# Queries and keys of a two-layer decoder computed with the tokens stationary, rotated as [tokens, columns] and turned through memory; other PSUM banks for the feed-forward

## The chip, the cores and the metric

The kernel runs on one core of one Trainium2 chip. The metric is the device time of one execution in microseconds (us), the median of several executions. A core has TensorE (PE, with a row of its own, PEld, for the loading of the stationary operand), VectorE (DVE), ScalarE (ACT), GpSimd (POOL) and SyncE (SP, which here does nothing but issue transfers).

## The reference, cut to what matters

Two layers over 256 tokens of width 2048, all float32. Each layer projects the normalised input to the q, k and v of four groups of 4 heads x 128, runs four kinds of causal attention on them, projects the result out and applies a SwiGLU feed-forward of width 5632.

```
for l in range(2):
    h = rmsnorm(x, attn_norm[l])
    z = h @ w_in[l]                      # q, k, v of fox, moba, diff, sb: 12 pieces of 512 columns, and 4 gate columns
    fox  = softmax(q k^T / sqrt(128) + gates, causal) v
    moba = softmax(rope(q) rope(k)^T / sqrt(128), causal) v
    diff = rmsnorm((softmax(rope(q1) rope(k1)^T / 8) - lam softmax(rope(q2) rope(k2)^T / 8)) v)
    sb   = stick_breaking(q, k) v
    x = x + concat(fox, moba, diff, sb) @ w_out[l]
    h = rmsnorm(x, ffn_norm[l])
    x = x + (silu(h @ w_gate[l]) * (h @ w_up[l])) @ w_down[l]
return rmsnorm(x, final_norm)
```

rope turns the two halves of a head (of half a head in diff) against each other: x1 cos - x2 sin and x2 cos + x1 sin.

## The kernel before

**Blocks.** All weights lie in memory as blocks of 128 x 1024 float32 (512 KB), in the order in which they are used. SP loads each into `raw` (L193, 4 buffers). ACT rounds it to `hi` (L202) and DVE forms the rest `lo = raw - hi` (L203), 3 buffers each; `run_ahead` does this for the two blocks after the current one. Activations have the same two halves (`xh`). Each product is three matmuls, hi by lo, lo by hi and hi by hi, in float32r.

**Products.** Three forms stand in the kernel. `rows_block` (L388, matmuls L399 to L401) holds 128 tokens stationary and streams 512 weight columns; it makes v, the output projection and most of the down projection, 12 matmuls of 512 columns to a block. `gate_up_product` (L405, matmuls at L417) does the same for gate and up. `pair_product` (L357, L369 to L371) makes q and k the other way round: 128 weight columns are stationary and the 256 tokens stream, 24 matmuls of 256 columns to a block, so that q and k come out as [columns, tokens], as the scores want them. There are 8 blocks to each of q, k and v of a group, so 16 q and k products in the two layers.

**Order.** A layer does v, q, k of diff, then q, k, v of moba, fox and sb, then the output projection, 11 chunks of gate and up, and the down projection. After each block `tick()` takes one step of three queues of side work, each written as a generator that yields between its steps: `evacs` (what empties PSUM), `background` (the attention of the groups, one group after the other) and `spare` (the forget gate). All engines work through their instructions in the order in which this program issues them. `OUT_ORDER` takes two blocks of the second output chunk ahead of the blocks that need the sb heads; if these aren't there, `source` finishes `background` on the spot.

**Emptying q and k.** `rope_pair` (L477) multiplies a pair of heads in PSUM by tables that already hold cos and sin times the norm's factor (`rope`, L351, made from a product with a diagonal, L327), and then combines the pieces in 8 (diff) or 4 (moba) small operations (L491, L492). `plain_pair` (L494) is one multiplication for fox and sb.

**Turning through memory.** `turn_steps` (L422) turns a [tokens, columns] result to [columns, tokens]: DVE transposes 32 x 32 pieces (L427), one step later SP writes 512 KB to memory (L430), two steps later SP reads it back in four transfers (L435), and two steps later it is used. Before the change this is done for the 22 chunks of act and the 14 of the output and down projections.

**PSUM.** Eight banks, four under the tag `mm` and four under `at`. The products take `mm`, the attention `at`. Gate and up alternate, chunk 0 in `mm` (L986: `("mm", "at")[c % 2]`); the norm's small sums are in `at`. So chunk 0 follows the last output product in `mm`, and the first down product follows chunk 10 in `mm`.

Of the kernel before, what the change touches and what calls it, by code (L numbers as in the profile page):

```python
# [19 lines left out]
P = 128  # L20
# [19 lines left out]
FG0 = 3 * GW  # L40
HEAD0 = {"fox": 0, "moba": 4, "diff": 8, "sb": 12}
# [7 lines left out]
def pair_columns(name, which, hp):  # L49

    c0 = COL0[name] + (0 if which == "q" else GW) + hp * 2 * HD
    base = c0 + np.arange(2 * HD).reshape(2, HD)
    if name == "moba":
        h = base.reshape(2, 2, 64)
        return h.transpose(1, 0, 2).reshape(-1)
    if name == "diff":
        h = base.reshape(2, 2, 2, 32)
        return h.transpose(2, 0, 1, 3).reshape(-1)
    return base.reshape(-1)
# [3 lines left out]
C_COS = {"moba": 0, "diff": 512}  # L63
C_ID = 1024
# [12 lines left out]
def constants():  # L77
    c = np.zeros((P, C_ALL), np.float32)
    pos = np.arange(S, dtype=np.float32)
    for name, dim in (("moba", HD), ("diff", HD // 2)):  # L80
        inv = (1.0 / (np.float32(10000.0) ** (np.arange(0, dim, 2, dtype=np.float32) / np.float32(dim)))).astype(np.float32)
        ang = (pos[:, None] * inv[None, :]).astype(np.float32)
        r = P // (dim // 2)
        c[:, C_COS[name]:C_COS[name] + S] = np.tile(np.cos(ang).T, (r, 1))
        c[:, C_COS[name] + S:C_COS[name] + 2 * S] = np.tile(np.sin(ang).T, (r, 1))
# [18 lines left out]
def lay_out(inp):  # L104
# [15 lines left out]
    for l in range(DEPTH):  # L120
# [9 lines left out]
        for kind, what, nb in plan():  # L130
            if what[0] != l:
                continue
            if kind == "pair":
                put(w_in, every, pair_columns(*what[1:]), 256)
            elif kind == "v":
                c0 = COL0[what[1]] + 2 * GW
                put(w_in, every, slice(c0, c0 + GW), 512)
# [21 lines left out]
def plan():  # L159

    out = []
    for l in range(DEPTH):
        for g in ORDER:
            pairs = [("pair", (l, g, which, hp), 4) for which in ("q", "k") for hp in range(2)]
            v = [("v", (l, g), 8)]
            out += v + pairs if g == ORDER[0] else pairs + v
# [8 lines left out]
def trunk(ctx: ExitStack, tc: tile.TileContext, x_t, vec, w, consts, y_t):  # L175
# [43 lines left out]
    for b, (to, of, c0, c1) in enumerate([(con, consts, C_ID, C_KEEP), (con, consts, 512, C_ID), (con, consts, 0, 512),  # L219
                                          (vecs, vec, V_GF, V_ALL)]):  # L220
        beside[NJ // 2 + b] = [(to[:, c0:c1], of[:, c0:c1])]
# [97 lines left out]
    def diag_product(cols):  # L319

        diag = tp.tile([P, 2, P], F32, name="diag", tag="diag", bufs=1)
# [8 lines left out]
    def norm_steps():  # L330
        acc = state["acc"]
        yield
        pst = ps.tile([P, 512], F32, name="pss", tag="at")
# [9 lines left out]
    def attn_norm_steps(l):  # L343
        yield from norm_steps()
        pbc = yield from diag_product(state["rcol"])
        rbc = tp.tile([P, S], F32, name="rbc", tag="rbc", bufs=1)
        A.activation(rbc, pbc[:, :S], AF.Copy)
        state["rbc"] = rbc
        rope = tp.tile([P, 4, S], F32, name="rope", tag="back", bufs=1)
        for n in range(4):  # L350
            V.tensor_tensor(rope[:, n], con[:, n * S:(n + 1) * S], rbc, op=ALU.mult)  # L351
        state["rope"] = {"moba": (rope[:, 0], rope[:, 1]), "diff": (rope[:, 2], rope[:, 3])}
# [4 lines left out]
    def pair_product(src):  # L357

        nonlocal block
        out = ps.tile([P, 2, S], F32, name="pp", tag="mm")  # L360
        for kb in range(4):
            run_ahead(block)
            hi, lo = halves.pop(block)
            for kk in range(4):
                k = kb * 4 + kk
                xk = src[k]
                for c in range(2):
                    at = kk * 256 + c * P
                    T.matmul(out[:, c], hi[:, at:at + P], xk[:, S:], start=k == 0 and c == 0, stop=False)  # L369
                    T.matmul(out[:, c], lo[:, at:at + P], xk[:, :S], start=False, stop=False)  # L370
                    T.matmul(out[:, c], hi[:, at:at + P], xk[:, :S], start=False, stop=k == NJ - 1 and c == 1)  # L371
            block += 1
            tick()
        return out

    def v_product():
        nonlocal block
        outs = [ps.tile([P, GW], F32, name=f"pv{t}", tag="mm") for t in range(2)]
# [43 lines left out]
    def turn_steps(get):  # L422
# [10 lines left out]
        back = tp.tile([P, 8, 4, 32], F32, name="back", tag="back", bufs=1)  # L433
# [43 lines left out]
    def rope_pair(name, out, hp, pp):  # L477
        cos, sin = state["rope"][name]
        both = tp.tile([P, 2, 2, S], F32, name="mcs", tag="tr", bufs=1)
        mc, ms = both[:, 0], both[:, 1]  # L480
        V.tensor_tensor(mc, pp, cos[:, None, :].to_broadcast([P, 2, S]), op=ALU.mult)
        V.tensor_tensor(ms, pp, sin[:, None, :].to_broadcast([P, 2, S]), op=ALU.mult)
        n = 64 if name == "moba" else 32
        yield
        for i in range(P // n):
            if i * n == 64:
                yield
            r = slice(i * n, (i + 1) * n)
            h = 2 * hp + i * n // 64
            to = 0 if name == "moba" else 64 * (i % 2)  # L490
            V.tensor_tensor(out[to:to + n, h], mc[r, 0], ms[r, 1], op=ALU.subtract)  # L491
# [583 lines left out]
```

## Time and profile before

| | before |
|---|---|
| median of 3 runs | 2290.41 us (2288.62 to 2291.55) |
| the profiled execution's own time | 2288.27 us |
| its span | 2286.5 us |
| granted TensorE clock, mean | 0.994 |
| PE busy | 2253.4 us (99%) |
| DVE busy | 1329.5 us (58%) |
| ACT busy | 1040.0 us (45%) |
| POOL busy | 224.3 us (10%) |
| moved by DMA | 456.47 MB, 200 GB/s |

The span is what the profiler saw of the program; 1.8 us of the execution's own time lie around it. Matmuls overlap each other, and their ends are modelled, so the time that one takes is read from the distance between the starts of two that follow each other, not from its own duration. Busy shares are means over the whole span; the attention, the output projection and the feed-forward have different limits.

### The profile page before, as it was taken

How to read it: one execution, taken by the hardware profiler on the slowest of the kernel's cores; microseconds unless marked ns; L12 is line 12 of the kernel's file. 1: busy time of each engine (PE TensorE's matmuls, PEld its weight loads, DVE VectorE, ACT ScalarE, POOL GpSimd, SP SyncE). 2: the span in 40 equal slices, each digit the busy share in tenths (PEclk: the TensorE clock that was granted, in tenths of full speed). 3: DMA queues.
4: the chain of work that ended last, by engine and by line, in shares of the span. 5: the costliest groups of instructions: out<-in, count | busy, mean ns of one | idle time of the engine just before them, and what ended most of it. 6: DMA issues, size and time to landing. Idle time of an engine off the chain costs nothing.

```text
span 2286.5 us, 30240 instructions
## 1 busy us (share of the span) xinstructions
PE 2253.4 (99%) x11801; PEld 1932.1 (85%) x11801; DVE 1329.5 (58%) x1524; ACT 1040.0 (45%) x1284; POOL 224.3 (10%) x206
## 2 busy tenths in 40 slices
PE   9999999999999999999999999999999999999997
PEld 7989988788888887888899899887888888878887
DVE  7995546555555555455569855565555555554444
ACT  6444454444444444444443444554444444444443
POOL 3570001100000000000007500010000000000001
PEclk9999999999999999999999999999999999999999
DMA  7554457667667666666654444576766766766673
GB/s 251 168 165 154 157 165 228 204 214 228 212 212 230 211 212 218 211 209 210 200 181 162 160 156 163 167 230 198 233 212 211 226 216 212 224 209 203 212 219 130
DMA packets 165744, 456.47 MB, mean 200 GB/s; under 512 B 15968, under 2 KB 53600, under 8 KB 165600
## 3 DMA queue, kind: packets, MB, share of 16 engines
q1 hardware_dynamic: 165168, 454.01, 62.5%
q8 instruction: 92, 1.51, 0.3%
q10 hardware_dynamic: 432, 0.53, 0.1%
q14 instruction: 52, 0.43, 0.1%
HBM read 433.50 MB, written 20.97 MB: 199 GB/s over the span
## 4 chain that ended last, share of the span: by engine, by line
PE 88%; DVE 7%; DMA 2%; issue 1%; ACT 1%; SPq 0%; DVEq 0%
PE gate L417 21%; PE up L417 21%; PE po L399 6%; PE po L400 6%; PE po L401 6%; PE pp L369 4%; PE pp L370 4%; PE pp L371 4%; PE po L458 3%; DVE lo L203 2%; PE pv L400 2%; PE pv L401 2%; PE pv L399 2%; PE po L459 1%; DMA back<-mem 1%
## 5 line engine op out<-in xcount | busy, mean ns | idle before, releaser
L203 DVE TENSOR_TENSOR lo<-raw,hi 128x1024 fp32r<-128x1024 f32 (+1 forms) x785 | 963.4, 1229 | 896.6 <-ACT hi L202 888.2
L202 ACT ACTIVATE hi<-raw 128x1024 fp32r<-128x1024 f32 (+1 forms) x785 | 829.6, 1059 | 1130.7 <-PE up L417 513.2
L417 PE MATMUL gate<-hi,xh 128*128 128x512 f32 x1408 | 550.5, 391 | 7.2 <-DVE tr L427 6.9
L417 PE MATMUL up<-hi,xh 128*128 128x512 f32 x1408 | 549.9, 391 | 0.0
L417 PEld LDWEIGHTS gate<-hi,xh 128*128 128x128 f32 x1408 | 265.6, 189 | 63.7 <-DVE tr L427 7.8
L417 PEld LDWEIGHTS up<-hi,xh 128*128 128x128 f32 x1408 | 265.5, 189 | 55.6 <-DVE tr L427 0.6
L369 PE MATMUL pp<-xh,hi 128*128 128x256 f32 x1024 | 292.4, 286 | 0.0
L370 PE MATMUL pp<-xh,lo 128*128 128x256 f32 x1024 | 289.9, 283 | 1.0 <-DVE lo L203 1.0
L371 PE MATMUL pp<-xh,hi 128*128 128x256 f32 x1024 | 289.7, 283 | 0.0
L417 PE MATMUL gate<-lo,xh 128*128 128x512 f32 x704 | 275.1, 391 | 1.1 <-DVE lo L203 1.1
L417 PE MATMUL up<-lo,xh 128*128 128x512 f32 x704 | 274.8, 390 | 0.0
L302 POOL TENSOR_TENSOR acc<-acc,sq 128x256 f32<-128x256 f32 x73 | 68.5, 938 | 1913.0 <-ACT sq L301 1910.3
L399 PE MATMUL po<-hi,act 128*128 128x512 f32 x528 | 205.6, 389 | 3.4 <-ACT g L964 3.4
L400 PE MATMUL po<-lo,act 128*128 128x512 f32 x528 | 205.4, 389 | 0.0
L401 PE MATMUL po<-hi,act 128*128 128x512 f32 x528 | 205.4, 389 | 0.0
L370 PEld LDWEIGHTS pp<-xh,lo 128*128 128x128 f32 x1024 | 196.4, 192 | 1.6 <-DVE lo L203 1.4
L369 PEld LDWEIGHTS pp<-xh,hi 128*128 128x128 f32 x1024 | 196.4, 192 | 0.2
L371 PEld LDWEIGHTS pp<-xh,hi 128*128 128x128 f32 x1024 | 196.3, 192 | 0.0
L417 PEld LDWEIGHTS gate<-lo,xh 128*128 128x128 f32 x704 | 132.8, 189 | 29.5 <-DVE lo L203 1.9
L417 PEld LDWEIGHTS up<-lo,xh 128*128 128x128 f32 x704 | 132.7, 189 | 27.5
L399 PEld LDWEIGHTS po<-hi,act 128*128 128x128 f32 x528 | 99.1, 188 | 24.8 <-ACT g L964 4.3
L401 PEld LDWEIGHTS po<-hi,act 128*128 128x128 f32 x528 | 99.1, 188 | 20.6
(225 smaller groups left out, 2391.8 us busy)
## 6 DMA issues: line engine op xcount, KB each, us to landing
raw<-w SPq DMA_DIRECT2D x783, 512.0 KB, 4.2
mem<-tr SPq DMA_DIRECT2D x36, 512.0 KB, 4.9
back<-mem SPq DMA_DIRECT2D x144, 128.0 KB, 4.7
x_all<-x_t SPq DMA_DIRECT2D x7, 256.0 KB, 6.9
y_t<-x_all SPq DMA_DIRECT2D x4, 256.0 KB, 3.0
con<-consts SPq DMA_DIRECT2D x3, 256.0 KB, 4.6
raw<-w SPq DMA_DIRECT2D x2, 256.0 KB, 3.5
y_t<-x_all SPq DMA_DIRECT2D x4, 128.0 KB, 2.3
```

Source lines behind the costliest of these rows:

```text
L202: A.activation(hi[:, c], raw[:, c], AF.Copy)
L203: V.tensor_tensor(lo[:, c], raw[:, c], hi[:, c].bitcast(F32), op=ALU.subtract)
L302: G.tensor_tensor(state["acc"], state["acc"], sq, op=ALU.add)
L369: T.matmul(out[:, c], hi[:, at:at + P], xk[:, S:], start=k == 0 and c == 0, stop=False)
L370: T.matmul(out[:, c], lo[:, at:at + P], xk[:, :S], start=False, stop=False)
L371: T.matmul(out[:, c], hi[:, at:at + P], xk[:, :S], start=False, stop=k == NJ - 1 and c == 1)
L399: T.matmul(outs[t], xlo, wh, start=first, stop=False)
L400: T.matmul(outs[t], xhi, wl, start=False, stop=False)
L401: T.matmul(outs[t], xhi, wh, start=False, stop=last)
L417: T.matmul(outs[n][t], st, wt[:, n * GC:(n + 1) * GC], start=first, stop=last)
L458: T.matmul(outs[n][c], hi[:, at:at + P], xk, start=k == 0, stop=False)
L459: T.matmul(outs[n][c][:, S:], lo[:, at:at + P], xk[:, :S], start=False, stop=end)
```

## The change

The 16 q and k products use `rows_block`, as v did, so they come out as [tokens, columns] in two PSUM banks, and `pair_product` is gone. `q_or_k_steps` empties them: for moba and diff four multiplications by the norm's factor and a table of cos or sin, and two operations that combine the halves; for fox and sb two ACT copies with the factor as scale. The result is turned by `turn_steps`. The operand that the scores hold stationary (q for fox, moba and diff, k for sb) is read back to `back` and copied by ACT to [head, token] order. The other is read back straight into its tile and streamed by the score matmuls through a pattern (`by_heads`) whose runs are 32 elements long, 128 elements apart. The product with a diagonal and the scaled tables are no longer made for the attention. The unscaled tables are larger: their three loads have 256, 256 and 512 KB in place of 256 KB each. In the feed-forward chunk 0 of gate and up, and so chunk 10 too, takes `at`, and the norm's sums take `mm`.

```diff
-    def pair_product(src):
...
-    def v_product():
-        nonlocal block
-        outs = [ps.tile([P, GW], F32, name=f"pv{t}", tag="mm") for t in range(2)]
+    def in_product():
+        outs = [ps.tile([P, GC], F32, name=f"in{t}", tag="mm") for t in range(2)]
         for kb in range(8):
             rows_block(x_source, outs, kb, 8)
         return outs
...
-    def rope_pair(name, out, hp, pp):
...
+    def q_or_k_steps(name, which, outs, to, ready):
+
+        z = tp.tile([P, 2, GC], F32, name="z", tag="g", bufs=1)
+        if name in TABLES:
+            at, n = TABLES[name]
+            halves_of = lambda a: a.rearrange("p (s h n) -> p s h n", h=2, n=n)
+            ms = tp.tile([P, 2, GC], F32, name="ms", tag="tr", bufs=1)
+            for m, out in enumerate((z, ms)):
+                for t in range(2):
+                    tab = con[:, at + (2 * m + t) * n:at + (2 * m + t) * n + n]
+                    V.scalar_tensor_tensor(out[:, t].rearrange("p (s n) -> p s n", n=n),
+                                           outs[t].rearrange("p (s n) -> p s n", n=n), state["rcol"][:, t:t + 1],
+                                           tab[:, None, :].to_broadcast([P, GC // n, n]), op0=ALU.mult, op1=ALU.mult)
+            yield
+            zh, mh = (a.rearrange("p t (s h n) -> p (t s) h n", h=2, n=n) for a in (z, ms))
+            V.tensor_tensor(zh[:, :, 0], zh[:, :, 0], mh[:, :, 1], op=ALU.subtract)
+            V.tensor_tensor(zh[:, :, 1], zh[:, :, 1], mh[:, :, 0], op=ALU.add)
         else:
-            V.scalar_tensor_tensor(out[:, 2 * hp:2 * hp + 2], pp, scale, rbc, op0=ALU.mult, op1=ALU.mult)
-        yield
+            r = state["rq" if which == "q" else "rcol"]
+            for t in range(2):
+                A.activation(z[:, t], outs[t], AF.Copy, scale=r[:, t:t + 1])
+        yield
+        if which == STATIONARY[name]:
+            new = yield from turn_steps(lambda t: z[:, t])
+            A.activation(to.rearrange("p h (a n) -> p h a n", n=32), new, AF.Copy)
+            yield
+        else:
+            yield from turn_steps(lambda t: z[:, t], to.rearrange("p h s -> p (h s)").rearrange("p (a h n) -> p a h n", h=NH, n=32))
+        ready[which] = True
...
-            T.matmul(s0[:, h], q[:, h, :P], k[:, h, :P], start=h == 0, stop=False)
+            T.matmul(s0[:, h], q[:, h, :P], k[:, h, :4], start=h == 0, stop=False)
...
             def pairs():
-                for which in ("q", "k"):
-                    for hp in range(2):
-                        pp = pair_product(xh)
-                        if name in ("moba", "diff"):
-                            evacs.append(rope_pair(name, qk[which], hp, pp))
-                        else:
-                            evacs.append(plain_pair(qk[which], hp, pp, HD ** -0.5 if which == "q" else None))
-                evacs.append(mark(ready))
+                for which in "qk":
+                    evacs.append(q_or_k_steps(name, which, in_product(), qk[which], ready))
...
-        evacs.append(norm_steps())
+        evacs.append(norm_steps("mm"))
         for c in range(NFC):
-            evacs.append(act_steps(c, *gate_up_product(("mm", "at")[c % 2])))
+            evacs.append(act_steps(c, *gate_up_product(("at", "mm")[c % 2])))
```

PE, early in the first q product of layer 0; `pp` and `in` are the product's PSUM tiles, `xh` the tokens, `hi` and `lo` the weights. Before:

```order
L369 MATMUL pp<-xh_118,hi_330 128x256
L370 MATMUL pp<-xh_118,lo_331 128x256
L371 MATMUL pp<-xh_118,hi_330 128x256
L369 MATMUL pp<-xh_125,hi_330 128x256
L370 MATMUL pp<-xh_125,lo_331 128x256
L371 MATMUL pp<-xh_125,hi_330 128x256
```

After:

```order
L371 MATMUL in_377<-hi_330,xh_118 128x512
L372 MATMUL in_377<-lo_331,xh_118 128x512
L373 MATMUL in_377<-hi_330,xh_118 128x512
L371 MATMUL in_378<-hi_330,xh_118 128x512
L372 MATMUL in_378<-lo_331,xh_118 128x512
L373 MATMUL in_378<-hi_330,xh_118 128x512
```

Before, the 256 tokens of a tile `xh` stream past 128 weight columns and then past the next 128 (the first three rows are the second half of `xh_118`); after, 128 tokens of it are held while all 512 weight columns stream, and then the other 128.

PE, output projection of layer 0, from the last products of the sb attention (`po<-t,v`) to the next weight block; `mix0` to `mix7` are the mixed heads, `mix6` and `mix7` those of sb. Before:

```order
L558 MATMUL po_3525<-t0_3299,v_2709 128x256
L559 MATMUL po_3525<-t1_3300,v_2709 128x128
L399 MATMUL po0_3443<-hi99_3483,mix3_2482 128x512
L400 MATMUL po0_3443<-lo99_3484,mix3_2482 128x512
L401 MATMUL po0_3443<-hi99_3483,mix3_2482 128x512
L399 MATMUL po1_3444<-hi99_3483,mix3_2482 128x512
```

After:

```order
L536 MATMUL po_2888<-t0_2672,v_2087 128x256
L537 MATMUL po_2888<-t1_2673,v_2087 128x128
L371 MATMUL po0_2688<-hi104_2822,mix6_2893 128x512
L372 MATMUL po0_2688<-lo104_2823,mix6_2893 128x512
L373 MATMUL po0_2688<-hi104_2822,mix6_2893 128x512
L371 MATMUL po1_2689<-hi104_2822,mix6_2893 128x512
```

Before, a block that reads the heads of another group (`mix3`) follows the sb products, and `mix6` is first read after several more; after, the block that follows reads `mix6`, which ACT and DVE make from those very products. Between the matmuls that finish the sb scores, which three Exp operations of ACT then read, and these products stand two weight blocks before the change and one after it.

SP, in the q and k products of layer 0: weight loads alone before,

```order
L193 DMA raw_1168<-w 128x1024
L193 DMA raw_1209<-w 128x1024
L193 DMA raw_1249<-w 128x1024
L193 DMA raw_1294<-w 128x1024
L193 DMA raw_1331<-w 128x1024
```

and after, with the k of diff being turned:

```order
L190 DMA raw_813<-w 128x1024
L402 DMA mem<-tr 128x2x512
L190 DMA raw_837<-w 128x1024
L190 DMA raw_859<-w 128x1024
L408 DMA k<-mem 32x8x128 x4
L190 DMA raw_885<-w 128x1024
```

The write `mem<-tr` and the four reads `k<-mem` now stand in the queue of the weight loads, two loads apart.

## Rows read from the trace of the kernel before

**Rows 1.** The page, part 1: busy time, share of the span, instructions.
```profile
PE 2253.4 (99%) x11801; PEld 1932.1 (85%) x11801; DVE 1329.5 (58%) x1524; ACT 1040.0 (45%) x1284; POOL 224.3 (10%) x206
```

**Rows 2.** Waits of PE: who waited for whom, total us, times, longest us.
```profile
PE gate L417 <- DVE tr L427: 6.9, 2, 3.5
PE pv L400 <- DVE lo L203: 3.8, 4, 1.4
PE po L399 <- ACT g L964: 3.4, 2, 1.7
```

**Rows 3.** Timeline, PE, 20 to 39 us: start, us, what was run.
```profile
20.25 0.39 PE L401 MATMUL pv<-hi,xh 128*128 128x512 f32 x1
...
31.13 0.39 PE L401 MATMUL pv<-hi,xh 128*128 128x512 f32 x1
...
33.07 0.28 PE L369 MATMUL pp<-xh,hi 128*128 128x256 f32 x1
...
38.35 0.28 PE L371 MATMUL pp<-xh,hi 128*128 128x256 f32 x1
```

**Rows 4.** Timeline, PE, start of the feed-forward of layer 0.
```profile
412.84 0.40 PE L417 MATMUL up<-hi,xh 128*128 128x512 f32 x1
416.70 0.80 PE L417 MATMUL gate<-hi,xh 128*128 128x512 f32 x1 [3.46 <-DVE tr L427]
...
422.57 0.40 PE L417 MATMUL up<-hi,xh 128*128 128x512 f32 x1
```

**Rows 5.** Windows: stretch, PE, PEld, DVE, ACT, POOL busy, granted clock, DMA.
```profile
416.70:422.20 5.50, 5.50 (x13) 4.17 (x14) 1.76 (x2) 1.06 (x1) 0.00 (x0) 0.50 0.75 255
```

**Rows 6.** Timeline, DVE, the same place as rows 4.
```profile
413.67 2.35 DVE L203 TENSOR_TENSOR lo<-raw,hi 128x1024 fp32r<-128x1024 f32 x2
415.94 1.30 DVE L427 STREAM_TRANSPOSE tr<-po 128x512 f32<-128x512 f32 x2
```

**Rows 7.** Timeline, PE, end of gate and up of layer 0.
```profile
897.24 0.39 PE L417 MATMUL up<-hi,xh 128*128 128x512 f32 x1
899.35 0.50 PE L399 MATMUL po<-hi,act 128*128 128x512 f32 x1 [1.72 <-ACT g L964]
```

**Rows 8.** Groups by form, DVE: busy us, mean ns, idle before.
```profile
L481 DVE TENSOR_TENSOR mcs<-pp,rope 128x512 f32<-128x512 f32 x16 | 10.9, 681 | 0.0
L491 DVE TENSOR_TENSOR q<-mcs 64x256 f32<-64x256 f32 x8 | 5.3, 663 | 0.1
L965 DVE SCALAR_TENSOR_TENSOR g<-up,rcol,g 128x512 f32<-128x512 f32 x44 | 30.9, 744 | 1.6 <-ACT g L964 1.6
L427 DVE STREAM_TRANSPOSE tr<-g 128x512 f32<-128x512 f32 x44 | 28.5, 687 | 0.0
```

**Rows 9.** Windows: a stretch of the attention of layer 0.
```profile
100.00:145.00 45.00, 42.26 (x314) 38.69 (x313) 44.24 (x71) 21.05 (x44) 41.91 (x35) 1.00 0.43 141
```

**Rows 10.** Timeline, stick-breaking group of layer 0, its last steps.
```profile
324.31 0.60 ACT L806 ACTIVATE t<-z 128x512 f32<-128x512 f32 x1
...
330.10 0.60 PE L558 MATMUL po<-t,v 128*128 128x256 f32 x2
...
331.19 0.38 PE L559 MATMUL po<-t,v 128*128 128x128 f32 x2
331.22 0.68 DVE L565 TENSOR_TENSOR mix<-po,mix 128x512 fp32r<-128x512 f32 x1
```

**Rows 11.** Waits (ACT and SP), then the DMA issues of the page.
```profile
ACT act L973 <- DMA back<-mem: 15.6, 14, 2.6
...
SPq L435 <- DMA mem<-tr: 19.8, 24, 2.6
...
back<-mem SPq DMA_DIRECT2D x144, 128.0 KB, 4.7
```

**Rows 12.** Groups by form, ACT.
```profile
L973 ACT ACTIVATE act<-back 128x512 fp32r<-128x512 f32 x44 | 27.3, 621 | 15.8 <-DMA back<-mem 15.6
...
L788 ACT ACTIVATE h<-n 128x512 fp32r<-128x512 f32 x2 | 1.2, 614 | 0.0
```

More of the change, by code (lines that the diff above doesn't have):

```diff
@@ L40 @@
 FG0 = 3 * GW
+STATIONARY = {"fox": "q", "moba": "q", "diff": "q", "sb": "k"}
 HEAD0 = {"fox": 0, "moba": 4, "diff": 8, "sb": 12}
@@ L46, in turned, with columns @@
     return np.arange(n).reshape(n // GC, 4, 4, 32).transpose(0, 2, 1, 3).reshape(-1)
[L49 to L64, printed above, removed]
+def columns(name, which):
+    c0 = COL0[name] + "qkv".index(which) * GW
+    order = np.arange(GW)
+    if which != "v":
+        order = order.reshape(NH, 4, 32).transpose(1, 0, 2).reshape(-1)
+    return c0 + order
+TABLES = {"moba": (0, 256), "diff": (1024, 128)}
+C_ID = 1536
 C_ONE = C_ID + P
@@ L132, in lay_out @@
                 continue
[L133 to L137, printed above, removed]
+            if kind == "in":
+                put(w_in, every, columns(*what[1:]), GC)
             elif kind == "out":
@@ L163, in plan @@
         for g in ORDER:
-            pairs = [("pair", (l, g, which, hp), 4) for which in ("q", "k") for hp in range(2)]
-            v = [("v", (l, g), 8)]
-            out += v + pairs if g == ORDER[0] else pairs + v
+            out += [("in", (l, g, which), 8) for which in ("vqk" if g == ORDER[0] else "qkv")]
         out += [("out", (l, c, kb), 1) for c, kb in OUT_ORDER]
@@ L344, in attn_norm_steps @@
         yield from norm_steps()
[L345 to L352, printed above, removed]
-    block = 0
-    def pair_product(src):
-        nonlocal block
[L360 to L374, printed above, removed]
-    def v_product():
-        nonlocal block
-        outs = [ps.tile([P, GW], F32, name=f"pv{t}", tag="mm") for t in range(2)]
+        rq = tp.tile([P, 2], F32, name="rq", tag="rq")
+        V.tensor_scalar(rq, state["rcol"], HD ** -0.5, None, op0=ALU.mult)
+        state["rq"] = rq
+    block = 0
+    def in_product():
+        outs = [ps.tile([P, GC], F32, name=f"in{t}", tag="mm") for t in range(2)]
         for kb in range(8):
@@ L420, in gate_up_product, with turn_steps @@
         return outs
-    def turn_steps(get):
+    def turn_steps(get, back=None):
         tr = tp.tile([P, 2, GC], F32, name="tr", tag="tr", bufs=1)
@@ L432, in turn_steps @@
         yield
-        back = tp.tile([P, 8, 4, 32], F32, name="back", tag="back", bufs=1)
+        if back is None:
+            back = tp.tile([P, 8, 4, 32], F32, name="back", tag="back", bufs=1)
         for g in range(4):
@@ L475, in tmp @@
         return big.tile(shape, dtype, name=name, tag=f"t{n}")
-    def rope_pair(name, out, hp, pp):
[L478 to L483, printed above, removed]
-        yield
-        for i in range(P // n):
-            if i * n == 64:
-                yield
[L488 to L491, printed above, removed]
-            V.tensor_tensor(out[to + n:to + 2 * n, h], mc[r, 1], ms[r, 0], op=ALU.add)
@@ L679, in score_steps @@
                 qu, ku = units[n * i + c]
-                T.matmul(s0[i][:, c], qu[:, :P], ku[:, :P], start=c == 0, stop=False)
+                T.matmul(s0[i][:, c], qu[:, :P], ku[:, :4], start=c == 0, stop=False)
         for c in range(n):
@@ L765, in sb_steps @@
         for h in range(NH):
-            T.matmul(z1[:, h], k[:, h, P:], q[:, h, P:], start=h == 0, stop=h == NH - 1)
+            T.matmul(z1[:, h], k[:, h, P:], q[:, h, 4:], start=h == 0, stop=h == NH - 1)
         yield
@@ L852, in attention @@
             at = 3 * (n % 2)
-            qk = {"q": tmp(at, [P, NH, S], "q"), "k": tmp(at + 1, [P, NH, S], "k")}
+            qk = {which: tmp(at + i, [P, NH, S], which) for i, which in enumerate("qk")}
             vt = tmp(at + 2, [P, 2, GW], "v")
@@ L857, in v_part @@
             def v_part():
-                outs = v_product()
+                outs = in_product()
                 if n:
@@ L891, in v_steps, with by_heads @@
         yield
-    def mark(ready):
-        ready["qk"] = True
-        yield
+    def by_heads(name, which, a):
+        if which == STATIONARY[name]:
+            return a
+        return a.rearrange("p h s -> p (h s)").rearrange("p (a h n) -> p h a n", h=NH, n=32)
     def group_steps(l, name, qk, ready):
-        while "qk" not in ready:
+        while "q" not in ready or "k" not in ready:
             yield
-        yield from STEPS[name](l, qk["q"], qk["k"], ready)
+        yield from STEPS[name](l, *(by_heads(name, which, qk[which]) for which in "qk"), ready)
     def add_to_x(c, po, gain):
```

36 lines of the change are left out of this document (15 added, 21 removed).

## The prediction

> **What bounds the kernel now.** I read the page first: TensorE (PE) is busy for 2253.4 of 2286.5 us, 99% [rows 1]. So the time is the number of matmuls times the distance between them, plus the few places where PE waits. The second view is the list of PE's waits. It is short: 6.9 us where the first gate product waits for VectorE transposes, in two events of at most 3.5 us, 3.8 us for late `lo` halves, and 3.4 us where the first down product waits for ACT to empty a gate bank, again in two events [rows 2]. There is one of each of the first and the third in a layer. The third view is PE's timeline, read for the starts. Between the starts at 20.25 and 31.13 lie 48 matmuls of 512 columns, so one takes 0.2267 us; between 33.07 and 38.35 lie 44 of 256 columns, so one takes 0.1200 us [rows 3]. Twice 256 columns cost 0.2400 us, 13.3 ns more than 512 at once.
>
> **The products.** 3072 matmuls of 256 columns become 1536 of 512 (16 products, 8 blocks each, 24 and 12 to a block). 3072 x 0.1200 = 368.6 us, 1536 x 0.2267 = 348.2 us: **20.5 us less**. The new form is that of v, whose rows I used for it, in the same stage of the kernel, so I see no bound other than the reading of the rows.
>
> At this term a rule speaks against the change. The Trainium skill, "TensorE: Matmul & The Clock Gate", section "Wait — 56ns, not 53.3ns?", gives the distance of warm matmuls as the columns at 2.4 GHz plus some 2.5 ns. By it the pairs would save an estimated 1536 x 2.5 ns, 3.8 us, and the sum below would be 16.7 us higher. Here the fixed part is 13.3 ns on both sizes [rows 3], so the trace disagrees with the rule and I go by the rows.
>
> **The start of the feed-forward.** In layer 0 PE starts a matmul at 412.84 and could start the next at 413.07. It starts at 416.70, since its `mm` bank still holds the last output product [rows 4]. The transposes that free it are queued on VectorE behind two `lo` operations and end at 417.24 [rows 6]; the first of the two frees the bank PE asks for. After this gap the granted clock is 0.50, the 1.2 GHz level [rows 5]: the 13 matmuls that start from 416.70 up to 422.57 take 5.87 us, not 13 x 0.2267 = 2.95 us [rows 4]. With chunk 0 in `at`, whose last tenants are the attention's, emptied many blocks before, the wait of 3.63 us and the 2.92 us at the lower clock go, 6.55 us in a layer, **13.1 us** for both (I take layer 1 as equal, since its wait is [rows 2]). What is late next there? Without the gap the second weight block would start at 414.43 and need its `lo` a little later; the two `lo` that stand ahead of the transposes are done at about 414.9 and 416.0 [rows 6], in time. The `lo` behind the transposes would end at about 418.5, and its block starts at 419.9. So I expect nothing in the gap's place; what it costs if I am wrong is rival 2.
>
> **The start of the down projection.** PE starts at 897.24 and could go on at 897.47; it goes on at 899.35 [rows 7]. Chunk 10 in `at` leaves `mm` to the down product: 1.88 us in a layer, **3.8 us**. Nothing else is asked for there.
>
> **What is added on VectorE and ACT** is hidden behind PE, as long as `lo` and `hi` stay ahead. A pair of moba heads cost VectorE two multiplications of 0.68 us and four combinations of at most 0.66 us, about 4.0 us; a product has two pairs, 8.0 us. After, it has four multiplications like the one from PSUM with a per-token scalar, 0.744 us, two combinations of 512 columns and two transposes of 0.69 us each: 5.7 us [rows 8]. That is less. But the cover is thin in one place. From 100 to 145 us, where the diff attention, the forget gate and moba's q and k meet, VectorE is busy for 44.24 of 45 us [rows 9], and there two of the late `lo` cost PE up to 1.4 us each [rows 2]. After the change the q and k of moba leave VectorE some 4.6 us less work there, but the 16 blocks that it has for them pass 16 x (24 x 0.1200 - 12 x 0.2267) = 2.6 us sooner, and the four multiplications now come in one step, 3.0 us, where the old steps had 1.4 to 2.6. I take the waits there as unchanged, 0, with bounds of 2.8 us less (the two waits of 1.4 gone) and 5.6 us more (twice as many again). ACT's copies (two to a product for fox and sb, one for the stationary side) run on an engine that is half idle in that stretch [rows 9].
>
> **Turns through memory.** Each of the 16 products now makes a write and four reads, on the SP queue between the weight loads. The 36 turns that exist have the same steps, at the same distance in blocks. There SP held its queue for the write to land in 24 cases, 19.8 us in all, 2.6 at most, and ACT waited for the data in 14, at most 2.6 us [rows 11]; none of this appears among PE's waits [rows 2]. So the weight queue gets 0. One place is new: the k of diff is streamed by PE straight from what the transfer wrote, and the diff scores are issued in the very step in which it is called ready. PE comes there about a block after ACT would, so I take 0.5 us in a layer, **1.0 us more**, with bounds of 0 and 2 x 2.6.
>
> **Later attention.** The turn makes k of sb ready six blocks later, so the sb products now stand directly ahead of the block that reads their result. The Exp operations are 0.60 us each [rows 10], three of them fit under the one weight block (2.72 us) that is left between. But the second half of the products lasts from 330.10 to about 331.4, while the first half's evacuation is done at 331.90 [rows 10]: 0.5 us, with a `lo` that may stand in between 0.6, in both layers **1.2 us more** (bounds 0 and 4). That the diff products start about five blocks later has the slack of a serial queue behind it.
>
> **Strided streaming.** The score matmuls read runs of 32 elements. No PE row shows that. The nearest rows are ACT's: with such runs as source 128x512 takes 621 ns, without 614 [rows 12]. I take 0. The other bound, half speed: 7680 columns in two passes and two layers, 30720 columns at 0.1200 us for 256, 14.4 us more.
>
> **The sum.** 2288.3 (the profiled execution) - 20.5 - 13.1 - 3.8 + 1.0 + 1.2 = 2253.1. The median of the three runs is 2.1 us above the profiled execution, while the diagonal product that goes is worth a little on the other side; I forecast **2254 us**. A change is told from none from 0.2% on, 4.6 us.
>
> **Rivals.**
> 1. *VectorE decides in the attention.* The four multiplications in one step, next to the softmax operations, stop PE for longer than the 1.4 us seen, and long enough that the clock falls as in rows 5. For it speaks the 98% of rows 9, against it that the work is less. With 2.8 us of waits and 2.9 us of lower clock more in each layer: 2265 us.
> 2. *The gap only moves.* If `hi` and `lo` are late as soon as the bank isn't, the 13.1 us come back by half or whole: 2261 to 2267. Against it stands the timetable of rows 6.
> 3. *Strided streaming at half speed:* 2268 us.
> 4. *The fixed part isn't won back:* the q and k matmuls of 512 columns stand 0.2400 us apart, as two of 256 do now, and the 20.5 us don't come: 2274. The v rows of rows 3, at 0.2267, speak against it. The rule of the Trainium skill's page "TensorE: Matmul & The Clock Gate" would put the time near there, at an estimated 2271.
> 5. *The other side: turns hold the weight queue until PE starves.* The write waits for the transposes, the reads for the write, and the weight loads stand behind both; in the attention VectorE is the late engine. The 16 turns undo the gain of 35 us from 2.2 us each on. If each cost 2.6 us for the write and 0.9 for late transposes, 16 x 3.5 = 56 us, the time would be 2310. For it speaks rows 11, against it that PE didn't wait at any of the 36.
>
> **How the numbers follow.** My forecast has 0.74, rival 1 0.09, rival 2 0.07, rival 3 0.03, rival 4 0.03, rival 5 0.03, and 0.01 lies with small losses that cancel the gain. Around the forecast the bounds of VectorE (-2.8 to +5.6), of diff's k (-1 to +4.2) and of sb (-1.2 to +2.8) and the spread of the runs give 2247 to 2262. Rivals 1 and 2 reach up to 2265, so I state 2247 to 2265. Faster: all but rival 5 and the rest, 0.96; same 0.01; slower 0.03.
>
> **What would show it.** PE starts 0.227 us apart in all q and k products and no 256-column ones; no wait of the first gate product for transposes and no clock of 0.50 at the start of the feed-forward; no wait of the first down product; an instruction wait of half a microsecond on `mix` in the output projection; waits of the diff scores on the transfer of k. The prediction is wrong if PE waits for `lo` or `hi` in the attention for more than 8 us in all, if the weight loads become a releaser of ACT there, or if the score matmuls stand further apart than before.

## The result, and the profile after

The changed kernel takes 2260.89 us, the median of 4 runs (2256.87 to 2265.54), beside 2289.51 us for the kernel before in the same measurement: ratio 0.9875, 95% interval 0.9853 to 0.9897, 28.6 us less. Two later measurements (e0 and e8 below) gave 2256.33 and 2257.52 us (ratios 0.9859 and 0.9864). The forecast was 2254, its range 2247 to 2265.

The page of the profiled execution (2259.36 us in all), from its first lines and from the DMA part:

```profile
span 2257.6 us, 27200 instructions
...
PE 2231.4 (99%) x10257; PEld 1848.3 (82%) x10257; DVE 1301.5 (58%) x1450; ACT 1056.1 (47%) x1306; POOL 227.8 (10%) x206
...
DMA packets 187491, 473.31 MB, mean 210 GB/s; under 512 B 17248, under 2 KB 71264, under 8 KB 187360
```

PE is still busy for 99%; its busy time is 22.0 us shorter [rows 1], and 17 MB more are moved, nearly all of it by the turns. What PE waited for, in us, times and longest:

```profile
PE in L372 <- DVE lo L200: 6.0, 12, 1.1
PE s L658 <- DMA k<-mem: 4.0, 4, 2.1
PE in L371 <- ACT hi L199: 1.9, 2, 1.3
...
PE po L371 <- DVE mix L543: 0.8, 2, 0.4
PE po L372 <- DVE lo L200: 0.8, 1, 0.8
PE gate L389 <- DVE lo L200: 0.4, 1, 0.4
```

The two large waits at the ends of the feed-forward [rows 2] are gone. PE's timeline where the feed-forward of layer 0 starts shows the same place as [rows 4]:

```profile
403.64 0.39 PE L372 MATMUL po<-lo,mix 128*128 128x512 f32 x1
403.87 0.39 PE L373 MATMUL po<-hi,mix 128*128 128x512 f32 x1
404.09 0.39 PE L389 MATMUL gate<-hi,xh 128*128 128x512 f32 x1
404.32 0.39 PE L389 MATMUL up<-hi,xh 128*128 128x512 f32 x1
404.55 0.39 PE L389 MATMUL gate<-lo,xh 128*128 128x512 f32 x1
```

The last output product and the first gate product now stand 0.22 us apart, and the granted clock from 400 to 408 us is 1.00. In their place a wait is on the list that was not there: the diff scores (`s`, L658) wait for the transfer of k. PE's timeline there, in layer 1:

```profile
1213.20 0.39 PE L372 MATMUL in<-lo,xh 128*128 128x512 f32 x1
1213.43 0.39 PE L373 MATMUL in<-hi,xh 128*128 128x512 f32 x1
1215.91 0.66 PE L658 MATMUL s<-k,q 64*128 64x128 f32 x2 [2.09 <-DMA k<-mem]
1217.11 1.19 PE L658 MATMUL s<-k,q 64*128 64x128 f32 x6 [0.53 <-DMA k<-mem]
1218.23 0.61 PE L661 MATMUL s<-mq_bf,id_bf 128*128 128x128 bf16 x4
1218.60 0.78 PE L371 MATMUL in<-hi,xh 128*128 128x512 f32 x1
...
1220.02 0.63 PE L371 MATMUL in<-hi,xh 128*128 128x512 f32 x1
1220.45 0.63 PE L372 MATMUL in<-lo,xh 128*128 128x512 f32 x1
...
1222.94 0.39 PE L372 MATMUL in<-lo,xh 128*128 128x512 f32 x1
```

and, by stretches, the busy times of PE, PEld, DVE, ACT and POOL, the granted clock, the DMA share and GB/s:

```profile
1195.00:1210.00 15.00, 14.72 (x63) 11.28 (x62) 15.00 (x21) 5.33 (x6) 14.21 (x9) 1.00 0.60 199
...
1216.00:1223.00 7.00, 6.47 (x23) 5.08 (x24) 4.04 (x6) 0.00 (x0) 6.43 (x7) 0.51 0.50 174
```

From the start at 1213.43 to the next product of the following block at 1218.60 pass 5.17 us; where k is there in time (run e9 below) it is 1.17. So 4.0 us are lost there. Of these 2.6 are the two waits; much of the rest is the lower clock already, since the six scores behind the second wait take 1.19 us, and 0.68 at the same place of layer 0. Behind the scores the clock is at its 1.2 GHz level: the 10 matmuls from 1218.60 to 1222.94 take 4.34 us, not 2.27, another 2.1. In layer 0 the same place loses 1.8 us (99.63 to 102.64) and 1.7 behind it (the 11 matmuls from 102.64 to 106.83 take 4.19 us, not 2.49). Together 9.6 us where the prediction had 1.0.

### The profile page after: what moved, and what is told of

The parts are those of the page before. It is cut to its first block, busy times and chain, and to the rows that moved or that the text cites. A ratio compares the mean times of both kernels' runs of the same rounds, so it can differ in the third digit from the quotient of the medians.

```text
span 2257.6 us, 27200 instructions
## 1 busy us (share of the span) xinstructions
PE 2231.4 (99%) x10257; PEld 1848.3 (82%) x10257; DVE 1301.5 (58%) x1450; ACT 1056.1 (47%) x1306; POOL 227.8 (10%) x206
## 4 chain that ended last, share of the span: by engine, by line
PE 90%; DVE 4%; DMA 3%; ACT 2%; issue 1%; SPq 0%; DVEq 0%; ACTq 0%
PE gate L389 21%; PE up L389 21%; PE po L371 7%; PE po L372 7%; PE po L373 7%; PE in L372 6%; PE in L371 6%; PE in L373 6%; PE po L431 3%; DVE lo L200 2%; PE po L432 1%; DMA raw<-w 1%; ACT hi L199 1%; DMA back<-mem 1%; DMA k<-mem 1%
## 5 line engine op out<-in xcount | busy, mean ns | idle before, releaser
L372 PE MATMUL in<-lo,xh 128*128 128x512 f32 x768 | 302.1, 393 | 6.1 <-DVE lo L200 6.0
L371 PE MATMUL in<-hi,xh 128*128 128x512 f32 x768 | 305.2, 397 | 2.0 <-ACT hi L199 1.9
L373 PE MATMUL in<-hi,xh 128*128 128x512 f32 x768 | 300.8, 392 | 0.0
L372 PEld LDWEIGHTS in<-lo,xh 128*128 128x128 f32 x768 | 145.3, 189 | 40.4 <-DVE lo L200 11.8
L371 PEld LDWEIGHTS in<-hi,xh 128*128 128x128 f32 x768 | 145.2, 189 | 32.2 <-ACT hi L199 3.4
L373 PEld LDWEIGHTS in<-hi,xh 128*128 128x128 f32 x768 | 145.0, 189 | 30.4
```

The lines of the kernel that those rows point to most:

```text
L371: T.matmul(outs[t], xlo, wh, start=first, stop=False)
L372: T.matmul(outs[t], xhi, wl, start=False, stop=False)
L373: T.matmul(outs[t], xhi, wh, start=False, stop=last)
```

## Experiments

My theory after this: the term for diff's k was far too small, and the rest came as worked out. The rival: other terms are off as well, above all VectorE's, and hide each other. Runs of one group shared a chip and the runs of the kernel before.

**First group: the k of diff, and the banks.** e0 is the change once more.

> The changed kernel once more, beside the next three on one chip. Both theories: a ratio to before near the 0.9875 measured, that is about 2261 us, and PE waits of the diff scores on k<-mem in both layers (4.0 us in its profile) with a granted clock of 0.50 right behind them.

e1 lets the diff attention start one step later:

```diff
         while "q" not in ready or "k" not in ready:
             yield
+        for _ in range(1 if name == "diff" else 0):
+            yield
```

> Only the diff attention starts one step of the side queue (one weight block, 2.72 us) later. Theory A (the diff scores wait for the transfer of k, and the clock falls after it): in the profile of the changed kernel PE lost 3.6 us at that place in layer 0 and 6.1 us in layer 1; the wait of 1.3 us in layer 0 goes, that of some 2.5 us in layer 1 goes or nearly, and with both the clock of 0.50: 7 to 10 us less than the changed kernel, 2251 to 2254 us. Theory B (the 7 us missing against the forecast lie in late lo and hi halves in the attention or in the spread of the runs): within 2 us of the changed kernel.

e2 calls diff's k ready one step sooner, the reads staying where they are:

```diff
-    def turn_steps(get, back=None):
+    def turn_steps(get, back=None, wait=2):
...
-        yield
-        yield
+        for _ in range(wait):
+            yield
         return back.rearrange("p a k n -> p k a n")
```

where the turn of diff's k is called with `wait` 1.

> The other direction: the k of diff is called ready one step earlier, so its scores are issued one weight block (2.72 us) sooner behind the same transfer. Theory A: PE waits one block more in each layer, 5.4 us, and the clock stays low for as long in layer 0 as in layer 1 (1.7 us more): 5 to 8 us over the changed kernel, 2266 to 2269 us. Theory B: no change beyond 2 us.

e3 puts the banks of the feed-forward and of the norm's sums back:

```diff
-        evacs.append(norm_steps("mm"))
+        evacs.append(norm_steps())
...
-            evacs.append(act_steps(c, *gate_up_product(("at", "mm")[c % 2])))
+            evacs.append(act_steps(c, *gate_up_product(("mm", "at")[c % 2])))
```

> The changed kernel with the PSUM banks of before in the feed-forward (chunk 0 of gate and up in mm, the norm's sums in at). The forecast's two terms: the wait of the first gate product for the transposes with the clock of 0.50 after it comes back (6.55 us in a layer) and the wait of the first down product (1.88 us in a layer): 16.9 us over the changed kernel, 2278 us. The rival that the gap had only moved: less than 8 us.

| run | median, us (runs) | ratio to before, 95% |
|---|---|---|
| e0, the change | 2256.33 (4) | 0.9859, 0.9844 to 0.9873 |
| e1, scores one step later | 2253.40 (4) | 0.9843, 0.9830 to 0.9856 |
| e2, scores one step sooner | 2270.01 (4) | 0.9913, 0.9901 to 0.9926 |
| e3, old banks | 2272.21 (6) | 0.9922, 0.9907 to 0.9937 |

In e1 the wait for k is gone, and the granted clock is 1.00 from 20 to 2240 us. But it is only 2.9 us faster than e0, and their intervals overlap. In e0's profile layer 0 waits for k for just 0.52 us and keeps its clock, layer 1 for 3.1. The wait has no fixed size. e2 shows that its edge is steep: with the waits at 7.0 us (one of 4.0) a step less costs 13.7 us, more than I expected. e3 costs 15.9 us, and the two waits return with their old sizes, 6.8 and 3.4 us: the banks are worth nearly the 16.9 us of the prediction. (The six runs of e3 lie far apart, from 2264.80 to 2277.00 us.)

**Second group: the other terms one by one.** e4 is e1 again, as the base.

> The kernel of the earlier run of that name once more, as the base of the two runs beside it. Theory A (the wait for diff's k and the lower clock behind it are all that this step takes away, and both vary in size from execution to execution): 2252 to 2256, no wait of a score matmul for the transfer, no stretch with a granted clock of 0.50 near 100 or 1215 us. Rival B (the first measurement was low by chance): about 2257 to 2261, the time of the change.

e5 issues each q and k matmul of e4 as two of 256 columns on the same stationary tokens:

```diff
-                T.matmul(outs[t], xlo, wh, start=first, stop=False)
-                T.matmul(outs[t], xhi, wl, start=False, stop=False)
-                T.matmul(outs[t], xhi, wh, start=False, stop=last)
+                for p in range(parts):
+                    c = slice(p * GC // parts, (p + 1) * GC // parts)
+                    T.matmul(outs[t][:, c], xlo, wh[:, c], start=first and p == 0, stop=False)
+                    T.matmul(outs[t][:, c], xhi, wl[:, c], start=False, stop=False)
+                    T.matmul(outs[t][:, c], xhi, wh[:, c], start=False, stop=last and p == parts - 1)
```

> The run beside it, with each q and k matmul of 512 columns issued as two of 256 on the same stationary tokens: 3072 matmuls of 256 in place of 1536 of 512, nothing else. Theory A (the 20.5 us of the products are a fixed part of 13.3 ns that each matmul has): 20.5 us more than the run beside it, about 2274, with starts 0.120 us apart in q and k. Rival B (the gain came from elsewhere, from VectorE's lighter work in the attention or from holding the tokens): no more than 4 us more, about 2254 to 2258. The Trainium skill's page TensorE: Matmul & The Clock Gate, section Wait - 56ns, not 53.3ns?, would give an estimated 3.8 us more.

e6 gives e4's four multiplications by the tables two steps:

```diff
             for m, out in enumerate((z, ms)):
+                if m:
+                    yield
                 for t in range(2):
```

> The run two before it, with the four multiplications by the tables issued in two steps of two. Theory A (the waits of about 1.08 us for lo where moba's q and k are emptied, two in each layer, come from the four multiplications that stand ahead of a lo in one step): those four waits fall below 0.5 us each, 2 to 4 us less, about 2250 to 2252. Rival B (VectorE has too much work there in sum, and the waits only move by a block): the same sum of waits, within 1.5 us of the base.

e7 is the kernel before with the new banks alone (e3's edit the other way round).

> The kernel before with only the banks of the feed-forward and of the norm's sums as in the change; the products are as before. Theory A (the banks are worth their 13.1 + 3.8 us by themselves, the lower clock behind the gap included): 16.9 us less than the kernel before, about 2272, no wait of the first gate product for transposes, none of the first down product for act, no granted clock of 0.50 near 417 and 1547. Rival B (the gap only moves, since hi and lo are late as soon as the bank isn't): half comes back, 2278 to 2282, with waits of the gate product for hi or lo of 2 us and more.

| run | median, us (4 runs each) | ratio to before, 95% |
|---|---|---|
| e4, scores one step later | 2252.56 | 0.9834, 0.9819 to 0.9848 |
| e5, e4 with 256 columns | 2268.03 | 0.9902, 0.9885 to 0.9918 |
| e6, e4 with tables in two steps | 2254.23 | 0.9839, 0.9824 to 0.9854 |
| e7, before with new banks | 2275.43 | 0.9929, 0.9915 to 0.9944 |

In e5 the starts in PE's timeline stand 0.120 us apart, as in the kernel before [rows 3], though the tokens are now the stationary side:

```profile
60.00 0.28 PE L374 MATMUL in<-lo,xh 128*128 128x256 f32 x1
60.12 0.28 PE L375 MATMUL in<-hi,xh 128*128 128x256 f32 x1
60.24 0.28 PE L373 MATMUL in<-hi,xh 128*128 128x256 f32 x1
```

So the cost is one of the matmul's size, not of which side is held. The time is 15.5 us above e4, not 20.5. The Trainium skill, "TensorE: Matmul & The Clock Gate", section "Wait — 56ns, not 53.3ns?", would have put it at an estimated 3.8; the run disagrees with it, as the rows did. Part of the missing 5 us stands in the lists of waits: in e4 PE waits for `lo` and `hi` at the start of the feed-forward for 3.0 us, in e5 for 1.1, and in q, k and v for `lo` for 4.9 against 3.8. Here a faster PE catches up with the engines that feed it.

e7 is 16.3 us under the kernel before (forecast 16.9), with none of the two waits. e6 makes no difference that can be told: the four waits of 0.59 to 1.08 us where moba is emptied fall to between 0.15 and 0.34, but new ones stand a few blocks later (0.86 for `lo`, 0.46 for `p`, in both layers). VectorE's work there has not become less, and the wait has only moved.

**Third group.** e8 is the change once more.

> The changed kernel once more, as the base of the run beside it that moves only the reads. Theory A (the wait of the diff scores for k and the lower clock behind it come in sizes from 0.5 to 2.6 us a layer, by when the reads land): 2255 to 2261, with at least one wait of a score matmul for k of over 0.5 us. Rival B (the wait is a property of the first execution only): no such wait, about 2253.

e9 leaves the diff scores where they are, but issues the four reads of diff's k a step sooner:

```diff
         nc.sync.dma_start(mem.rearrange("t i r g n -> (i r) t (g n)"), tr)
-        yield
-        yield
+        for _ in range(2 - early):
+            yield
...
-        yield
-        yield
+        for _ in range(2 + early):
+            yield
```

where `early` is 1 for diff's k and 0 elsewhere.

> The changed kernel with the four reads of diff's k issued one step sooner, ahead of one weight block instead of behind two, the scores where they are. Theory A (the reads land late because two weight blocks of 512 KB are issued ahead of them on the same queue): k lands some 2 us sooner, the wait of the scores for it and the lower clock behind it are gone, 3 to 8 us less than the change, about 2253. Rival B (SP then stands for the write to land, and the weight blocks behind it are late): new waits of in for hi of 1 us and more, no gain, 2256 to 2262.

e10 adds VectorE work to e4, on a tile that nobody reads:

```diff
             V.tensor_tensor(zh[:, :, 1], zh[:, :, 1], mh[:, :, 0], op=ALU.add)
+            for _ in range(3):
+                V.tensor_tensor(ms[:, 0], ms[:, 0], ms[:, 1], op=ALU.add)
```

> The kernel with the diff attention one step later, and three more VectorE additions of 512 columns (0.68 us each) in the step that combines the halves, on a tile that nobody reads, in each of the 8 q and k products of moba and diff: 16.3 us of VectorE work, about the 2.3 us a product that the change takes away from it. Theory A (the lighter work of VectorE is worth several us, since lo is late where moba's q and k are emptied): 4 to 9 us more than that kernel without the additions, 2257 to 2262, in waits of in for lo in both layers. Rival B (VectorE's work there is covered, and only what stands directly ahead of a lo counts): within 2 us of it, 2251 to 2256.

e11 takes one more block of the second output chunk ahead in e4:

```diff
-OUT_ORDER = [(0, kb) for kb in range(6)] + [(1, 0), (1, 1), (0, 6), (0, 7)] + [(1, kb) for kb in range(2, 8)]
+OUT_ORDER = [(0, kb) for kb in range(6)] + [(1, 0), (1, 1), (1, 2), (0, 6), (0, 7)] + [(1, kb) for kb in range(3, 8)]
```

> The kernel with the diff attention one step later, and three blocks of the second output chunk in place of two ahead of the blocks that need sb. Theory A (the two waits of 0.39 us for the mixed heads are for want of time alone): they are gone, 0.8 to 1.5 us less than without, 2251 to 2253. Rival B (the wait is replaced by one for lo of the next block, as one of 0.76 us stood there in some runs): no difference, 2253 to 2255.

| run | median, us (runs) | ratio to before, 95% |
|---|---|---|
| e8, the change | 2257.52 (4) | 0.9864, 0.9849 to 0.9879 |
| e9, reads one step sooner | 2254.48 (4) | 0.9846, 0.9832 to 0.9859 |
| e10, e4 with more VectorE work | 2272.76 (5) | 0.9929, 0.9912 to 0.9947 |
| e11, e4 with one more block ahead | 2257.90 (4) | 0.9860, 0.9846 to 0.9873 |

e9 and e8 together show what k is late behind. SP's timeline in layer 0 and, in the last row, the median us from issue to landing (from 86 to 103 us), in e8:

```profile
89.08 0.38 SPq L402 DMA_DIRECT2D mem<-tr  x1
90.59 2.35 SPq L190 DMA_DIRECT2D raw<-w  x2
92.98 1.90 SPq L408 DMA_DIRECT2D k<-mem  x4
...
k<-mem SPq DMA_DIRECT2D x4, 128.0 KB, 7.5
```

and the same in e9:

```profile
87.68 0.38 SPq L402 DMA_DIRECT2D mem<-tr  x1
89.42 0.33 SPq L190 DMA_DIRECT2D raw<-w  x1
91.56 1.81 SPq L408 DMA_DIRECT2D k<-mem  x4
93.46 8.83 SPq L190 DMA_DIRECT2D raw<-w  x5
...
k<-mem SPq DMA_DIRECT2D x4, 128.0 KB, 3.5
```

Counted from the write, the reads are issued at nearly the same time (3.9 us after it in both). What differs is what is on its way ahead of them: two weight blocks, issued in the 2.4 us before, in e8, and one, issued 2.1 us before, in e9. The reads land in 7.5 against 3.5 us. The Trainium skill, "DMA: Bandwidth & Descriptors", section "Queues, rings and completion order", says that each DMA engine takes the descriptors of a ring in their order; the two landings agree with it.

The number of blocks ahead is not the whole reason. The k of moba has two ahead of it as well, and lands sooner. SP in e8, layer 0, with its landing, and then the landing of the block directly ahead of the reads, first at diff's k (issued at 92.60) and then at moba's (147.69):

```profile
145.07 2.95 SPq L190 DMA_DIRECT2D raw<-w  x2
148.07 1.90 SPq L408 DMA_DIRECT2D k<-mem  x4
...
k<-mem SPq DMA_DIRECT2D x4, 128.0 KB, 4.1
...
raw<-w SPq DMA_DIRECT2D x1, 512.0 KB, 7.0
raw<-w SPq DMA_DIRECT2D x1, 512.0 KB, 3.8
```

At both places the first of the four reads lands 0.6 us behind that block. So the landing follows the block directly ahead, and at diff's k this block itself is slow, 7.0 us where the median of all blocks in e8 is 4.2. What slows it, no run here shows.

In e9's PE timeline the scores follow at once:

```profile
98.20 0.39 PE L373 MATMUL in<-hi,xh 128*128 128x512 f32 x1
98.52 0.71 PE L659 MATMUL s<-k,q 64*128 64x128 f32 x8
99.17 0.40 PE L662 MATMUL s<-mq_bf,id_bf 128*128 128x128 bf16 x4
99.37 0.47 PE L371 MATMUL in<-hi,xh 128*128 128x512 f32 x1
```

The gain is 3.0 us against e8, which waits for k for 5.4 us; the intervals overlap, as with e0 and e1. e9 has 1.6 us of waits for `p` in moba that e8 has for 0.2, and 2.6 us at the start of the feed-forward for `hi` and `lo` that e8 has for 0.2. So in these two profiles part of what is saved at k is lost again further on. One such place can be followed in e4, on VectorE, ACT and PE, where the output projection of layer 1 ends:

```profile
1510.55 1.23 DVE L902 TENSOR_TENSOR x_all<-x_all,back 128x1024 f32<-128x1024 f32 x1 [3.34 <-DMA back<-mem]
...
1511.81 0.51 ACT L303 ACTIVATE xh<-x_all,vecs 128x256 fp32r<-128x256 f32 x1 [5.86 <-DVE x_all L902]
...
1514.33 0.50 PE L389 MATMUL gate<-hi,xh 128*128 128x512 f32 x1 [1.32 <-ACT hi L199]
```

Another read-back (issued from 1501.97, landing after 7.1 us at the median) holds VectorE, VectorE holds ACT, and the `hi` queued behind four small operations on ACT comes 1.32 us late. That is read from the trace; no run removed it.

e10: the list of PE's waits of the base e4, and then of e10:

```profile
PE in L372 <- DVE lo L200: 4.9, 7, 1.1
...
PE s L658 <- DMA k<-mem: 0.2, 1, 0.2
```

```profile
PE in L372 <- DVE lo L200: 19.8, 17, 3.7
PE po L372 <- DVE lo L200: 1.7, 3, 0.8
```

The additions take 931 ns each at the mean, not 680, and VectorE is busy for 17.6 us more than in e4. They cost about 20 us (ratio 0.9929, against 0.9834 and 0.9843 for the kernel without them, on other chips), more than twice what I expected. Part of this is the clock: in the profile the granted clock falls to 0.50 three times, at 92.2, 122.9 and 1218.6 us, where e4 keeps it. So at this dose work added on VectorE in the attention is paid in full by PE; that work taken away would come back in full is not shown.

e11 fails: the wait for `mix` is 0.39 us in both layers, as before the edit, and the time is no better (ratio 0.9860, against 0.9834 and 0.9843 for the kernel without the edit, on other chips). PE's timeline in e11 says why the wait stays:

```profile
336.18 0.60 PE L536 MATMUL po<-t,v 128*128 128x256 f32 x2
336.61 0.38 PE L537 MATMUL po<-t,v 128*128 128x128 f32 x2
337.38 0.50 PE L371 MATMUL po<-hi,mix 128*128 128x512 f32 x1 [0.39 <-DVE mix L543]
```

The sb products are issued on the spot when the block that needs them comes up, and so always stand directly ahead of it; a block taken ahead moves both.

## Why the prediction was right, and where not

The time lies in the range, and the direction and most of the size came from the mechanisms named. That the forecast came within 2.3 to 6.9 us of the three measurements is in part luck: the products gave 5.0 us less than worked out, diff's k cost 2 us more, and a gain that is not in the sum made up for it. Where the time went can be read by stages, cut at the starts of two kinds of ACT operations: the emptying of diff's v, and the first Silu of a layer.

| us, profiled executions | to v, layer 0 | to Silu | to v, layer 1 | to Silu | to the end |
|---|---|---|---|---|---|
| before | 45.6 | 419.3 | 700.3 | 429.9 | 691.5 |
| e7, new banks only | 44.8 | 412.8 | 698.3 | 425.3 | 689.6 |
| e5, 256 columns, k in time | 43.5 | 413.6 | 697.8 | 422.1 | 688.7 |
| e4, 512 columns, k in time | 43.1 | 405.7 | 697.8 | 415.5 | 688.8 |
| after | 43.2 | 407.5 | 697.8 | 420.5 | 688.7 |
| e10, more VectorE work | 42.6 | 419.7 | 697.8 | 426.3 | 688.1 |

- **The feed-forward's banks, 13.1 + 3.8 us: right.** e7 gives 16.3 and e3 15.9. Layer 0 of e7 has 6.5 us less in the stage with the first gate product (forecast 6.55) and 2.0 less in the next (1.88); layer 1 has 4.6 and 1.9. In layer 1 the profiled execution of e7 lost some time to a lower clock in the attention, which the kernel before did not (last section). No wait took the gap's place: rival 2 fell.
- **The products, 20.5 us: the mechanism right, the gain 15.5.** The distances of the starts are as read, 0.2267 and 0.120, so rival 4 fell. What PE gains per product, it passes on in part as waits for `lo` and `hi`: between e5 and e4 the two attention stages shrink by 7.9 and 6.6 us, not by 10.2 each. Of the missing 5.9 the waits on the lists account for 3.1. Added up over all starts of PE in the two traces, the time from a q, k or v matmul to the next matmul is 557.9 us in e5 and 540.0 in e4, 17.9 less; so about half of what is missing lies in the products themselves, and about as much behind them, above all where the output projection ends and the feed-forward starts (2.0).
- **VectorE's 0: not settled.** The prediction had both sides, 4.6 us less work and blocks that pass 2.6 us sooner, and set them equal. The runs show a gain that the sum did not have: e5, which has as many matmuls at the same distance as e7, is 7.4 us faster (5.0 in the profiled executions), with 2.9 us of waits for `lo` in the attention where e7 has 6.2 for `lo` and `p`. That VectorE's lighter work is the cause is not shown. The two kernels differ in the tables, the turns and the order of the attention too; by the stages e5 is not faster in the attention of layer 0 (413.6 against 412.8), and in layer 1 e7 has the lower clock. Rival 1 did not happen, but e10 shows how near it lay: 2 us more work in each of eight products, and VectorE decides.
- **Diff's k, 1.0 us: the step that failed.** I took the landing of all read-backs, 4.7 us at the median [rows 11], and gave the scores 0.5 us a layer. At this place the reads stand behind weight blocks that are still on their way, and land in 6.5 us in layer 0 and 7.7 in layer 1 of the profile after; and I charged no lower clock behind the wait, though rows 5 had shown one. Locally it costs 9.6 us in the profiled execution. Taken away it gives back 2.9 (e1) and 3.0 us (e9), each within the noise by itself but both the same way, and e2 makes it worse by a clear 13.7. Two things may be why so little comes back: in e9 3.8 us of other waits appear, for `p` in moba and for `hi` and `lo` at the start of the feed-forward, and the wait is smaller in e0 than in this execution. Neither is shown as the cause. So the term is some 3 us as the kernel stands, still inside the bound of 5.2.
- **Late sb, 1.2 us: right in place and kind,** two waits of 0.39 us for `mix`, against 0.6 each.
- **Strided streaming, 0: right.** The 128x256 score matmuls take 378 ns at the mean, before and after, but such ends are modelled. The starts say the same: from the first of eight diff scores of 256 columns to the product behind them pass 1.07 us before (92.28 to 93.35) and 1.06 after (107.15 to 108.21), so rival 3 fell. Rival 5 fell as well: SP waited 24.6 us in all for writes to land, in 31 cases, and no transfer of weights is on PE's list. But a sign of it is there that the prediction had listed among those of being wrong: ACT, which before waited for a weight block at the start of the kernel alone, does so in e8 at both places of the diff scores too (2.45 us at 99.67, 2.07 at 1214.51). PE stood for k there anyway.

The steps from before over e7 and e5 to e4 (16.3, 7.4 and 15.5 us) were measured in one group, so their sum, 39.2 us, is simply the distance of e4 from the kernel before there; less the 3.0 us of k it would be 36.2 for the change. The three measurements of the change have 28.6, 32.6 and 33.1. This is no contradiction: the same kernel with the scores one step later is 35.5 us under the kernel before in the first group (e1) and 39.2 in the second (e4), so the groups differ by as much. But it is no closed account either. The change's first four runs vary more than those of the kernel before (2256.87 to 2265.54, against 2287.76 to 2291.55), which agrees with a wait whose size hangs on when a transfer lands; but e1, without the wait, also spreads over 5.1 us, so this is not shown.

The best version measured is the change with its diff attention one step later (e1, e4: 2253.40 and 2252.56 us), some 3 us under the change; with the reads a step sooner (e9) it is 2254.48, which can't be told from it.

## What to carry to other kernels

Where PE reads directly what a transfer brings, price the landing from the place itself, by what is still on its way ahead of it, and not from a median over all places; try to issue the read ahead of a bulk load rather than behind it (here 3.5 us to landing, not 7.5). When PE is made faster, engines that were just in time become late (here 15.5 us came of 20.5 worked out from PE's distances): ask for the busy share of the feeders in that stretch. Removing one wait in such a stretch can be worth less than its length (here 5.4 us of listed waits for 3.0).

## What was not expected of the hardware

The granted clock fell to 0.50 behind rather short waits: in layer 0 of the profile after two of 1.12 and 0.23 us were enough, and in layer 0 of e0 one of 0.52 was not. In e8 it fell behind waits of 2.21 and 0.78 us in layer 0, but not behind 1.72 and 0.72 in layer 1. Not even equal waits do the same: in e7 each layer has one of 0.48 us for `p` and, 2 us later, one of 1.40 for `lo`, and the clock falls in layer 1 alone. The stretches behind them, in layer 0 and in layer 1, with 14 and with 8 matmuls of PE in 3.4 us:

```profile
143.70:147.10 3.40, 3.34 (x14) 2.48 (x15) 3.34 (x5) 0.62 (x1) 3.22 (x3) 1.00 0.51 152
1265.50:1268.90 3.40, 3.40 (x8) 2.72 (x9) 3.34 (x5) 0.00 (x0) 3.22 (x3) 0.50 0.50 154
```

So the loss that follows a wait is not a fixed one, and it can be nearly as large as the wait (1.7 us behind 1.8 in layer 0 of the profile after, 2.1 behind 4.0 in layer 1).
